# A two-layer hybrid decoder trunk on one core: gate and branch products token-major, weight prefetch raised in steps, a planner that orders by data dependencies, and the two parts of x side by side

## The chip, the core and the metric

The kernel runs on one core of one Trainium2 chip. The metric is the time of one execution on the device in microseconds (us). A core has a matrix engine (TensorE, "PE" in the profile, with its weight loads as "PEld"), a vector engine (VectorE, "DVE"), an activation engine (ScalarE, "ACT"), GpSimd ("POOL") and SyncE ("SP"), whose queue here issues nearly all DMAs. Each engine works through its own instructions in order; engines wait for one another through semaphores.

## The reference

Two layers, each a token mixer and a SwiGLU feed-forward part, on 256 tokens of 1024 channels, all in float32. What the change touches is the mixer's input projection (its merge gates), the three branch products and the output product:

```python
proj = jnp.einsum("bsd,de->bse", x, w_in)
...
gates = jax.nn.sigmoid(p_merge + gate_b).reshape(Bsz, S, N_BRANCH, D)
merged = sum(gates[:, :, gi] * jnp.einsum("bsc,cd->bsd", y, w_branch[gi])
             for gi, y in enumerate((ya, yb, yc)))
return jnp.einsum("bsd,de->bse", merged, w_out).astype(x.dtype)
...
x = _layer_norm(alpha * x + mix, ln1_g[l], ln1_b[l])
h = jax.nn.silu(jnp.einsum("bsd,df->bsf", x, w1)) * jnp.einsum("bsd,df->bsf", x, w3)
```

The branches are a gated linear recurrence (A), a chunked gated delta rule with a triangular solve (B) and chunked gated linear attention (C). `p_merge` has 3 x 1024 columns, each branch product is 512 by 1024.

## The kernel before

**Precision and weights.** A float32 product is made of three matmuls on values split in a high and a low part: high x high, high x low, low x high. Weights come in units of 128 x 1024 values (512 KB); `load_w` fetches a unit into one of 4 `raw` tiles over SP's queue, `split_w` makes the parts (`hi` by ACT, `lo` by DVE), and `unit` hands them to the matmuls. `fill` keeps `ahead[0]` units split ahead of use: 6, and 14 (`FAR`) from the first product of branch B on. All larger tiles share 37 slots of 128 x 1024 values (`slot`); PSUM is 8 banks of 128 x 512 values (`bank`).

**Two shapes of product.** Feature-major (`fm_acc`, output tile `fm` or `br`): the weights are stationary, the 256 tokens move, one matmul writes 128 features by 256 tokens. Token-major (`tm_acc`, output `tm`, `wo`, `w`): 128 tokens are stationary and 512 columns of weights move. Both do the same arithmetic per unit: 24 matmuls of 256 columns or 12 of 512. In the feed-forward part `fm_acc2` (output `f13`, named `f` in the trace) takes the high weights once for both parts of x, as 512 moving columns in two runs of 256 that lie 512 values apart (`xtile`, order q, k, c), and then the low weights with 256 columns.

**The mixer's order** stands in `MIX`. The units before the gates make the inputs of the branches. Each gate unit pair (`gA0` and so on, 4 for each branch, `fm_pair` with `g_chain`) ends in two sigmoids on ACT that read PSUM and add the bias as a per-partition operand. Each branch unit (`bA0`, with `m_chain`) ends in a product with its gate and a sum into `macc` on DVE; the last branch splits `macc` straight into `mh`, which the output product `wo` then uses as stationary operand, since it is feature-major already. Between these units stand the short steps of the chains (`b_inv`, `a_chain`, `c_chain`): a few small matmuls (`px`, `pp`, `pt`, `pw`, ...), then a copy or a product on ACT or DVE, and so on.

**What sets the order.** `Order` keeps a clock for each engine with a cost for each operation, and `drive` takes the next step of a chain as soon as its inputs are ready by these clocks, or else the next unit of the main stream. Within one step an operation is taken to wait for all that the other engines did in this step. ACT's functions that need a table (`TABLES`) are held in this order; a change of table costs an `ACT_TABLE_LOAD`.

Of the kernel before, what the change touches and what calls it, by code (L numbers as in the profile page):

```python
# [33 lines left out]
V_AW, V_AB, V_BR, V_BI, V_LAM, V_BW, V_BN, V_CG, V_CN, V_GB, V_AL, V_SM = (  # L34
    0, 16, 20, 24, 28, 32, 80, 81, 83, 84, 108, 112)
NV = 113
# [5 lines left out]
MIX = ("c0 c1 ax0 k0 k1 q0 z0 q1 ax1 v0 v1 ag0 ag1 gA0 gA1 gA2 gA3 bA0 bA1 bA2 bA3 "  # L42
       "gC0 bC0 gC1 bC1 gC2 bC2 gC3 bC3 gB0 gB1 bB0 bB1 gB2 bB2 gB3 bB3").split()
# [4 lines left out]
def stream_order():  # L48
# [5 lines left out]
    for u in MIX:  # L54
        nm, i = u[:-1], int(u[-1])
        if nm == "z":
            o += tm(C_Z)
        elif nm in base:
            o += fm(base[nm], i)
        else:  # L60
            b = "ABC".index(nm[1])
            o += fm(C_MG + 1024 * b, i) if nm[0] == "g" else [("br", b, i)]
    o += [("wo", n, q) for n in range(2) for q in range(4)]
# [11 lines left out]
def pack(inp):  # L75
# [3 lines left out]
    for l in range(L):  # L79
        w_in = a["w_in"][l]  # L80
        for i, u in enumerate(ORDER):
# [5 lines left out]
            elif u[0] == "br":  # L87
                src, sh = a["w_branch"][l, u[1]][:, 256 * q:256 * q + 256], (4, P, 256)
# [21 lines left out]
    for l in range(L):  # L110
# [11 lines left out]
        v[:, V_GB:V_GB + 24] = fm(a["gate_b"][l])  # L122
# [9 lines left out]
    for n, s in enumerate((8, 16)):  # L132
# [13 lines left out]
        "wg2": np.ascontiguousarray(a["c_w_g2"]),  # L146
        "lnv": np.ascontiguousarray(np.stack(
# [9 lines left out]
class Order:  # L157

    def __init__(self):
        self.clk = {e: 0.0 for e in ("pe", "act", "dve", "pool", "dma")}
        self.tok = {}
        self.chains = []
        self.table = "?"
        self.begin(0.0)

    def begin(self, ready):
        self.ready = ready
        self.fin = {}  # L170

    def op(self, eng, cost, ready=0.0):
        t = max([self.clk[eng], self.ready, ready] +
                [f for e, f in self.fin.items() if e != eng])
        t += cost
        self.clk[eng] = t
        self.fin[eng] = t
        return t

    def end(self):  # L180
        return max(list(self.fin.values()) + [self.ready])
# [67 lines left out]
def _build(ctx, nc, tc, ins, out):  # L249
# [33 lines left out]
    def act_fn(o, i, f, **k):  # L283
# [10 lines left out]
        O.op("act", 0.12 + 0.09 * aps + 0.000833 * n_of(o))  # L294
# [4 lines left out]
    def dve(o, x=0.0):  # L299
        O.op("dve", 0.13 + x + 0.00104 * n_of(o))  # L300

    def tt(o, a, b, op):
        V.tensor_tensor(out=o, in0=a, in1=b, op=op)  # L303
        dve(o)

    def ts(o, a, s1, op0, s2=None, op1=None):
# [4 lines left out]
        dve(o)  # L311

    def stt(o, a, s, b, op0, op1):
        V.scalar_tensor_tensor(out=o, in0=a, scalar=s, in1=b, op0=op0, op1=op1)
        dve(o, 0.06)

    def vcopy(o, i):
        V.tensor_copy(o, i)
        dve(o)

    def cpred(o, m, d):
        V.copy_predicated(o, m, d)
        dve(o)

    def rowsum(o, i):
        V.tensor_reduce(o, i, axis=AX.X, op=ADD)
        dve(i)

    def scan(o, a, b):
        V.tensor_tensor_scan(o, a, b, 0.0, MULT, ADD)  # L330
        dve(o, 0.00104 * n_of(o))

    def recip(o, i):
        V.reciprocal(o, i)
        dve(o, 0.0075 * n_of(o))

    def rsqrt(o, i, e):
        G.tensor_tensor(out=o, in0=i, in1=e, op=ALU.pow)
        O.op("pool", 0.3 + 0.17 * n_of(o))
# [5 lines left out]
    def mm(o, w, x, start=True, stop=True):  # L345
        T.matmul(o, w, x, start=start, stop=stop)  # L346
        n, m = n_of(x), n_of(w)
        if w.dtype == F32R:
            O.op("pe", max(n, m, 128) / 2400.0)
        else:  # L350
            O.op("pe", max(n, m, 32) / 600.0)

    def tp(o, i, idn):
        T.transpose(o, i, idn)  # L354
        O.op("pe", 0.107)
# [46 lines left out]
    def load_w(between=None):  # L402
# [5 lines left out]
        for c in halves(i):  # L408
            nc.sync.dma_start(out=t[:, c], in_=ins["w"][l, j][:, c])
            if i == 0 and c.start == 0:  # L410
                between()
        O.clk["dma"] = max(O.clk["dma"], O.clk["pe"] - 4.0) + 1.5
        raws.append((t, O.clk["dma"] + 2.0))

    def split_w(between=None):
        if not raws:
            return
        t, at = raws.pop(0)
        i = pos[1]
        pos[1] += 1  # L420
        keep = O.ready, O.fin
        O.begin(at)
# [8 lines left out]
        ready.append((hi, lo, O.end()))  # L431
        O.ready, O.fin = keep
        load_w()
# [7 lines left out]
    def unit(nk, hold=0):  # L441
# [4 lines left out]
        hi, lo, at = ready.pop(0)  # L446
        O.ready = max(O.ready, at)
# [5 lines left out]
    def fm_acc(o, w, x, c=slice(None)):  # L453

        nk = w[0].shape[1]
        for k in range(nk):
# [22 lines left out]
    def xtile(name):  # L479
        v = [slot(name, F32R).rearrange("p (q k c) -> p k q c", q=2, k=2) for _ in range(4)]  # L480
# [14 lines left out]
    def layer(l, xs, xtok):  # L495
# [507 lines left out]
        def g_chain(ps, b, j):  # L1003
            ps = p2(ps)
            if j % 2 == 0:
                B["gt", b, 0], B["gt", b, 1] = pair2("gt")
            gt = B["gt", b, j % 2]
            for t in range(2):
                act_fn(gt[:, t], ps[:, t], AF.Sigmoid, bias=vc(V_GB + 8 * b + 2 * j + t))
            B["gg", b, j] = gt  # L1010
            done(f"gt{b}{j}")
            return
            yield

        def m_chain(ps, n, b, j, mh, ml):
            yield k_(f"gt{b}{j}")
            ps = p2(ps)
            gt = B["gg", b, j]
            if n == 0:
                if j % 2 == 0:  # L1020
                    B["macc", j], B["macc", j + 1] = pair2("macc")
                tt(B["macc", j], ps, gt, MULT)
            else:
                tt(gt, ps, gt, MULT)
                tt(B["macc", j], B["macc", j], gt, ADD)
            if n == 2:
                split(mh[j], ml[j], B["macc", j])
                done(f"mrg{j}")

        def ln_chain(tk, halves, lv, xs_out, is_out, name):  # L1030
# [5 lines left out]
            for n, ps in enumerate(halves):  # L1036
# [5 lines left out]
                for c0 in range(sl.start, sl.stop, c):  # L1042
                    V.bn_stats(st[:, c0 // c], s[:, c0:c0 + c])
                    O.op("dve", 0.1 + 0.001 * c)
                c0 = sl.stop
            mv, rs = sm("mv", [P, 2]), sm("rs", [P, 1])
            V.bn_aggr(mv, st[:, 0:D // c].rearrange("p a b -> p (a b)"))
# [101 lines left out]
        def tm_group(x, chains, second):  # L1149


            if second is None:
                for chain in chains:
                    ps = [bank("tm") for _ in range(2)]
                    for q in range(4):
# [3 lines left out]
                        if q == 3:  # L1159
                            for tk in range(2):  # L1160
                                O.spawn(chain(ps[tk], tk), 1)
                        yield
                return
            u = []
            for tk in range(2):
                if tk:
                    yield second
                for n, chain in enumerate(chains):
                    ps = bank("tm")
                    for q in range(4):  # L1170
# [9 lines left out]
                        if q % 2:  # L1180
                            yield

        def fm_pair(chain, prio):
            ps = bank("fm")
            for t in range(2):
                fm_acc(p2(ps)[:, t], unit(8), xs)
                if t:
                    O.spawn(chain(ps), prio)
                yield

        def main():
# [17 lines left out]
            for u in MIX:  # L1209
# [11 lines left out]
                elif nm[0] == "g":  # L1221
                    b = "ABC".index(nm[1])
                    yield from fm_pair(lambda ps: g_chain(ps, b, i), 1)
                else:
                    n, b = BRANCHES.index(nm[1]), "ABC".index(nm[1])
                    if n == 2:
                        ahead[0] = FAR
# [3 lines left out]
                    w = unit(4)  # L1231
                    ps = bank("br")
                    for t in range(2):
                        fm_acc(p2(ps)[:, t], w, y, slice(P * t, P * t + P))
                    O.spawn(m_chain(ps, n, b, i, mh, ml), 1)
                    yield
# [18 lines left out]
            seq = [(n, q) for n in range(2) for q in range(4)]  # L1255
# [8 lines left out]
            for i in range(8 - tail):  # L1264
                yield k_(f"mrg{i}")
                w = unit(2)
                for tk in range(2):
                    wo(i, w, tk)
            u = []
            for tk in range(2):  # L1270
                for i in range(8 - tail, 8):
                    if tk == 0:
                        if i < 4:
                            yield k_(f"mrg{i}")
# [37 lines left out]
            for j in range(NF - tail):  # L1312
# [7 lines left out]
                yield  # L1320
# [25 lines left out]
    with tc.manual_schedule(engines={mybir.EngineType.SP}):  # L1346
# [9 lines left out]
        for q in range(4):  # L1356
            if q % 2 == 0:
# [3 lines left out]
            ld = [lambda c=c: nc.sync.dma_start(out=t[:, c:c + 3 - n],  # L1361
                                                in_=ins["xfm"][:, 2 * q + c:2 * q + c + 3 - n])
# [4 lines left out]
        nc.sync.dma_start(out=kc, in_=ins["kc"])  # L1367
        for l in range(L):
            nc.sync.dma_start(out=vecs[:, l], in_=ins["vec"][l])
# [4 lines left out]
        for l in range(L):  # L1374
            nc.sync.dma_start(out=wr[l], in_=ins["wsm"][l])
# [46 lines left out]
        def prep_aw(l):  # L1422
# [3 lines left out]
            for q in range(2):  # L1426
                ar = ars[q]
                G.memset(ar, 0.0)
                O.op("pool", 0.6)
                src = ins["aw"][l, q].rearrange("(c w) i j -> w i c j", w=2)  # L1430
                for w in range(2):
                    nc.sync.dma_start(out=h4(ar)[64 * w:64 * w + 64, :, 64 * w:64 * w + 64],
                                      in_=src[w])
            O.op("dma", 6.0)
# [5 lines left out]

        O.tok["xin"] = 0.0
# [18 lines left out]
```

## Time and profile before

| | us |
|---|---|
| median of 3 runs (lowest to highest) | 939.6 (938.99 to 940.14) |
| the profiled execution | 940.46 |
| its span, first to last instruction | 938.7 |
| PE busy in it | 924.4 |
| DVE busy | 642.0 |
| ACT busy | 527.6 |

The profile is of one execution. Busy times of PE are modelled and its matmuls overlap: the mean duration of a matmul is longer than the distance between two of them. The chain of waits gives a stretch of matmuls with its length and its count, and from that the distance. 1.8 us of the execution lie around the span.

### The profile page before, as it was taken

How to read it: one execution, taken by the hardware profiler on the slowest of the kernel's cores; microseconds unless marked ns; L12 is line 12 of the kernel's file. 1: busy time of each engine (PE TensorE's matmuls, PEld its weight loads, DVE VectorE, ACT ScalarE, POOL GpSimd, SP SyncE). 2: the span in 40 equal slices, each digit the busy share in tenths (PEclk: the TensorE clock that was granted, in tenths of full speed). 3: DMA queues.
4: the chain of work that ended last, by engine and by line, in shares of the span. 5: the costliest groups of instructions: out<-in, count | busy, mean ns of one | idle time of the engine just before them, and what ended most of it. 6: DMA issues, size and time to landing. Idle time of an engine off the chain costs nothing.

```text
span 938.7 us, 15760 instructions
## 1 busy us (share of the span) xinstructions
PE 924.4 (98%) x6306; PEld 840.3 (90%) x6306; DVE 642.0 (68%) x1017; ACT 527.6 (56%) x827; POOL 29.0 (3%) x29
## 2 busy tenths in 40 slices
PE   8999999999999999999999999999999999999996
PEld 5999999999988888888889999989999888888885
DVE  6778976675865776675557879574768658666715
ACT  5867679535724755565045864973457147555600
POOL 1000100000000000000000020000100000000001
PEclk9999999999999999999999999989999999999999
DMA  8855243545851865578144444234468248555801
GB/s 284 257 183 154 78 149 94 186 166 193 297 222 67 281 213 186 193 244 264 54 156 140 144 146 131 95 122 149 158 240 285 105 138 280 187 179 180 291 1 45
DMA packets 47993, 162.84 MB, mean 173 GB/s; under 512 B 7536, under 2 KB 8496, under 8 KB 47792
## 3 DMA queue, kind: packets, MB, share of 16 engines
q1 hardware_dynamic: 47776, 161.71, 51.5%
q8 instruction: 49, 0.80, 0.3%
q14 instruction: 24, 0.20, 0.1%
q10 hardware_dynamic: 144, 0.13, 0.0%
HBM read 160.77 MB, written 1.05 MB: 172 GB/s over the span
## 4 chain that ended last, share of the span: by engine, by line
PE 91%; ACT 4%; DVE 2%; DMA 1%; issue 1%; POOL 0%; SPq 0%; POOLq 0%; DVEq 0%; ACTq 0%
PE fm L346 25%; PE f L346 22%; PE w L346 13%; PE tm L346 11%; PE br L346 7%; PE wo L346 5%; DMA raw<-in_w_dram 1%; ACT L291 1%; PE pt L346 1%; PE pp L346 1%; DVE lo L303 1%; PE pln L354 1%; PE co L346 1%; ACT hi L291 1%; PE ptm L354 0%
## 5 line engine op out<-in xcount | busy, mean ns | idle before, releaser
L303 DVE TENSOR_TENSOR lo<-raw,hi 128x1024 fp32r<-128x1024 f32 (+1 forms) x293 | 350.8, 1217 | 94.4 <-ACT hi L291 88.1
L291 ACT ACTIVATE hi<-raw 128x1024 fp32r<-128x1024 f32 (+1 forms) x293 | 300.6, 1053 | 79.5 <-DMA raw<-in_w_dram 64.6
L346 PE MATMUL fm<-x,hi 128*128 128x256 f32 x1536 | 282.9, 286 | 0.0
L346 PEld LDWEIGHTS fm<-x,hi 128*128 128x128 f32 x1536 | 240.1, 192 | 2.3 <-issue 1.6
L346 PE MATMUL fm<-x,lo 128*128 128x256 f32 x768 | 217.6, 283 | 0.0
L346 PE MATMUL f<-x,hi 128*128 128x512 f32 x576 | 203.8, 399 | 0.0
L346 PE MATMUL f<-x,lo 128*128 128x256 f32 x576 | 161.8, 281 | 0.0
L346 PEld LDWEIGHTS fm<-x,lo 128*128 128x128 f32 x768 | 147.7, 192 | 0.0
L346 PEld LDWEIGHTS f<-x,hi 128*128 128x128 f32 x576 | 108.2, 188 | 26.9
L346 PE MATMUL w<-hi,hh 128*128 128x512 f32 (+1 forms) x396 | 111.1, 367 | 0.0
L346 PEld LDWEIGHTS f<-x,lo 128*128 128x128 f32 x576 | 108.8, 189 | 0.1
L346 PE MATMUL tm<-hi,x 128*128 128x512 f32 x320 | 100.7, 398 | 2.1 <-ACT hi L291 2.1
L346 PEld LDWEIGHTS w<-hi,hh 128*128 128x128 f32 x396 | 71.4, 189 | 12.3
L346 PEld LDWEIGHTS tm<-hi,x 128*128 128x128 f32 x320 | 59.3, 190 | 15.3 <-ACT hi L291 3.8
L346 PE MATMUL w<-lo,hh 128*128 128x512 f32 (+1 forms) x198 | 72.4, 366 | 0.0
L346 PE MATMUL tm<-lo,x 128*128 128x512 f32 x160 | 62.2, 392 | 0.1
L291 ACT ACTIVATE gt<-fm,vecs 128x256 f32<-128x256 f32 x48 | 20.5, 470 | 48.0 <-PE fm L346 48.0
L346 PEld LDWEIGHTS w<-lo,hh 128*128 128x128 f32 x198 | 37.3, 188 | 6.2
L291 ACT ACTIVATE x<-pln 128x256 fp32r<-128x256 f32 x24 | 7.9, 383 | 61.7 <-PE pln L354 61.7
L346 PE MATMUL wo<-hi,mh 128*128 128x512 f32 x128 | 39.8, 392 | 0.0
L303 DVE TENSOR_TENSOR hv<-f,hv 128x256 f32<-128x256 f32 x36 | 15.2, 422 | 31.4 <-ACT hv L291 31.4
L346 PEld LDWEIGHTS tm<-lo,x 128*128 128x128 f32 x160 | 30.2, 189 | 7.1 <-DVE lo L303 0.7
(276 smaller groups left out, 1081.8 us busy)
## 6 DMA issues: line engine op xcount, KB each, us to landing
raw<-in_w_dram SPq DMA_DIRECT2D x291, 512.0 KB, 4.4
lnv<-in_lnv_dram SPq DMA_DIRECT2D x8, 512.0 KB, 8.0
xr<-in_xtm_dram SPq DMA_DIRECT2D x1, 1024.0 KB, 7.4
xin<-in_xfm_dram SPq DMA_DIRECT2D x3, 256.0 KB, 7.0
raw<-in_w_dram SPq DMA_DIRECT2D x2, 256.0 KB, 3.4
ar<-in_aw_dram SPq DMA_DIRECT2D x8, 64.0 KB, 3.9
out_dram<-xr SPq DMA_DIRECT2D x2, 256.0 KB, 2.1
kc<-in_kc_dram SPq DMA_DIRECT2D x1, 476.0 KB, 8.9
```

What stands on the lines that cost most here:

```text
L291: ins_ = A.activation(o, i, f, **k)
L303: V.tensor_tensor(out=o, in0=a, in1=b, op=op)
L346: T.matmul(o, w, x, start=start, stop=stop)
L354: T.transpose(o, i, idn)
```

## The change

Gates and branch products become token-major: `gA0` is now 512 columns of gates for both halves of the tokens (4 units, 48 matmuls of 512 columns), `bA0` 512 columns of the product (2 units). `MIX` has two of each per branch in place of four. The gate's bias differs from column to column there, so that it is fetched as a tile of 128 equal rows (`gbias`, 512 KB, one for each branch and layer, on SP's queue) and added by DVE from PSUM; ACT then takes the sigmoid. The last branch's sum is token-major, and `m_tm` turns it by four matrix transposes for each half of the columns and of the tokens (`pmt`) before the split into `mh`. `wo` walks its units in the order of the columns of `mh`.

`ahead[0]` goes up by 1 at each unit of branch C and by 2 at each of branch B, and to 14 only at `wo`. `Order` now notes which part of which tile each operation reads and writes, so that an operation waits for its own inputs alone; its costs are new, an engine's occupation and the delay until a result can be read are kept apart, and DMA is counted by bytes. `fm_pair`, `tm_group` and the branch units yield after half a unit, so that chain steps can go between. `xtile` lays the parts of one block side by side (order k, q, c): `fm_acc2`'s 512 columns are now one run.

```diff
+MIX = ("c0 c1 ax0 k0 k1 q0 z0 q1 ax1 v0 v1 ag0 ag1 gA0 gA1 bA0 bA1 gC0 bC0 gC1 bC1 "
+       "gB0 gB1 bB0 bB1").split()
...
+            o += tm(C_MG + 1024 * b + 512 * i) if nm[0] == "g" else [
+                ("br", b, i, q) for q in range(2)]
+    o += [("wo", n, q) for q in range(4) for n in range(2)]
...
+    def op(self, eng, occ, tail=0.0, out=None, ins=(), ready=0.0):
+
+        t = max(self.clk[eng], self.ready, ready)
+        for a in ins:
+            t = max(t, self.after(eng, a, False))
+        if out is not None:
+            t = max(t, self.after(eng, out, True))
+        self.clk[eng] = t + occ
+        f = t + occ + tail
...
     def xtile(name):
-        v = [slot(name, F32R).rearrange("p (q k c) -> p k q c", q=2, k=2) for _ in range(4)]
+        v = [slot(name, F32R).rearrange("p (k q c) -> p k q c", q=2, k=2) for _ in range(4)]
...
+        def g_tm(ps, b, j, tk, bias):
+            if tk == 0:
+                B["gt", b, j] = pair("gt")
+            gt = B["gt", b, j][tk]
+            tt(gt, ps, bias[:, 512 * j:512 * j + 512], ADD)
+            yield
+            act_fn(gt, gt, AF.Sigmoid)
+            done(f"gt{b}{j}{tk}")
...
+            tt(gt, ps, gt, MULT)
+            acc = B["macc", tk][j]
+            tt(acc, acc, gt, ADD)
+            if n == 1:
+                return
+            yield
+            pt = h4(bank("pmt"))
+            for q in range(4):
+                tp(pt[:, q], acc[:, q * P:(q + 1) * P], ident)
+            for q in range(2):
+                split(*(x[2 * j + q][:, :, tk * P:(tk + 1) * P] for x in (mh, ml)),
+                      pt[:, 2 * q:2 * q + 2])
+            done(f"mrg{j}{tk}")
...
-                    yield from fm_pair(lambda ps: g_chain(ps, b, i), 1)
+                    if i == 0:
+                        bias = slot("gbias")
+                        nc.sync.dma_start(out=bias, in_=ins["gb"][
+                            l:l + 1, 1024 * b:1024 * b + 1024].to_broadcast([P, 1024]))
+                    yield from tm_group(xs, [
+                        lambda ps, tk: g_tm(ps, b, i, tk, bias)], None)
...
+                    if n == 1:
+                        ahead[0] = min(ahead[0] + 1, FAR)
                     if n == 2:
-                        ahead[0] = FAR
+                        ahead[0] = min(ahead[0] + 2, FAR)
```

How the instructions stand on three engines, before and after. First PE at the end of the mixer of layer 0 (`br`: last branch product, `ybh`: branch B's output, `wo`: the output product's four banks, `mh`: the merged sum). Before the change:

```order
L346 MATMUL br_3121<-ybh_2483,hi_2851 128x256 x2
L346 MATMUL br_3121<-ybh_2483,lo_2852 128x256
L346 MATMUL wo_3161<-hi_2857,mh_375 128x512 x2
L346 MATMUL wo_3161<-lo_2858,mh_375 128x512
L346 MATMUL wo_3161<-hi_2857,mh_375 128x512 x2
```

After it, at the same place:

```order
L389 MATMUL br_2651<-hi_2518,ybh_2233 128x512 x2
L389 MATMUL br_2651<-lo_2519,ybh_2233 128x512
L398 MATMUL pmt_2721<-kc_73,macc_2096 128x128 x4
L398 MATMUL pmt_2730<-kc_73,macc_2130 128x128 x4
L398 MATMUL pmt_2741<-kc_73,macc_2096 128x128 x4
L389 MATMUL wo_2713<-hi_2541,mh_377 128x512
L389 MATMUL wo_2715<-hi_2541,mh_377 128x512
L389 MATMUL wo_2714<-hi_2559,mh_377 128x512
L389 MATMUL wo_2713<-hi_2541,mh_377 128x512
L389 MATMUL wo_2713<-lo_2542,mh_377 128x512
```

The transposes of the last sums now stand between the last branch product and `wo`; the first matmuls of `wo` take three banks in turn. Then ACT in layer 1, where the recurrence of branch A (`th`, `a`, `r`, `v` and `gl` are its and branch B's inputs) meets the steps of the solve (`pb` and `X` are copies out of PSUM that the next small matmuls `pt` and `pp` wait for; `hi` is a weight split). Before:

```order
L291 ACTIVATE r_6441<-a_6443 128x512 x2
L291 ACTIVATE hi<-raw 128x1024
L291 ACTIVATE pb<-pp 128x512
L291 ACT_TABLE_LOAD
L291 ACTIVATE gt<-fm,vecs 128x256 x2
L291 ACTIVATE pb<-pp 128x512
L291 ACTIVATE hi<-raw 128x1024
L291 ACTIVATE gt<-fm,vecs 128x256 x2
L291 ACT_TABLE_LOAD
L291 ACTIVATE th<-th 128x512 x2
L291 ACTIVATE hi<-raw 128x1024
L291 ACTIVATE X<-px 128x512 x2
```

After it, at the same step of the solve:

```order
L331 ACTIVATE v<-fm,vecs 128x256 x2
L331 ACTIVATE hi<-raw 128x1024
L331 ACTIVATE pb<-pp 128x512 x2
L331 ACTIVATE th<-r_5845,nc_81 128x256 x4
L330 ACT_TABLE_LOAD
L331 ACTIVATE a_5847<-r_5845,nc_81 128x256 x4
L331 ACTIVATE r_5845<-a_5847 128x512 x2
L331 ACT_TABLE_LOAD
L331 ACTIVATE v<-v 128x512
L331 ACTIVATE hi<-raw 128x1024
L331 ACTIVATE X<-px 128x512 x2
L331 ACTIVATE hi<-raw 128x1024
```

Both copies of `pb` now stand together ahead of the loads of tables, and no gate's sigmoid (`gt`) stands in this stretch. Last SP's queue in layer 0 (`raw`: weight units, `ar`: small weights of the next layer). Before:

```order
L409 DMA raw<-in_w_dram 128x1024 x14
L1432 DMA ar<-in_aw_dram 64x4x64 x4
L409 DMA raw<-in_w_dram 128x1024 x35
L1432 DMA ar<-in_aw_dram 64x4x64 x4
L409 DMA raw<-in_w_dram 128x1024 x36
L1249 DMA xr<-in_xtm_dram 128x2048
```

After it, up to the fetch of `xr` again:

```order
L447 DMA raw<-in_w_dram 128x1024 x13
L447 DMA ar<-in_aw_dram 64x4x64 x4
L447 DMA raw<-in_w_dram 128x1024 x28
L1284 DMA gbias<-in_gb_dram 128x1024
L447 DMA raw<-in_w_dram 128x1024 x8
L447 DMA ar<-in_aw_dram 64x4x64 x4
L447 DMA raw<-in_w_dram 128x1024 x4
L1284 DMA gbias<-in_gb_dram 128x1024
L447 DMA raw<-in_w_dram 128x1024 x14
L1284 DMA gbias<-in_gb_dram 128x1024
L447 DMA raw<-in_w_dram 128x1024 x16
L1317 DMA xr<-in_xtm_dram 128x2048
```

Three fetches of `gbias` now stand between the weight units, each as the first gate of its branch begins.

## Rows read from the trace of the kernel before

**Rows 1.** The page: busy time per engine; shares of the chain by engine.

```profile
PE 924.4 (98%) x6306; PEld 840.3 (90%) x6306; DVE 642.0 (68%) x1017; ACT 527.6 (56%) x827; POOL 29.0 (3%) x29
...
PE 91%; ACT 4%; DVE 2%; DMA 1%; issue 1%; POOL 0%; SPq 0%; POOLq 0%; DVEq 0%; ACTq 0%
```

**Rows 2.** The chain, in order of time: start us, us, engine, output, count of matmuls.

```profile
32.48 2.88 PE fm L346 x24
...
113.47 0.87 PE px L354 x8
...
178.93 8.63 PE br L346 x72
...
222.98 11.52 PE fm L346 x96
...
257.54 19.97 PE wo L346 x88
...
309.72 96.10 PE f L346 x544
...
478.60 10.91 PE tm L346 x48
...
491.37 2.86 PE fm L346 x24
...
615.36 3.95 PE fm L346 x24
...
721.16 8.21 PE wo L346 x36
...
869.70 61.09 PE w L346 x330
```

**Rows 3.** Busy time by stretch: stretch, length, PE, PEld, DVE, ACT, POOL, PEclk, DMA.

```profile
92.70:120.00 27.30, 27.30 (x228) 26.82 (x227) 26.75 (x64) 17.76 (x33) 4.65 (x2) 1.00 0.31 110
120.00:150.00 30.00, 29.57 (x315) 28.92 (x315) 18.40 (x30) 25.92 (x45) 0.00 (x0) 1.00 0.33 98
150.00:257.50 107.50, 107.50 (x913) 107.10 (x913) 77.21 (x100) 63.62 (x86) 2.63 (x3) 1.00 0.60 201
580.00:616.00 36.00, 33.47 (x269) 32.98 (x268) 22.65 (x30) 32.41 (x50) 0.00 (x0) 0.93 0.37 122
616.00:656.00 40.00, 39.94 (x407) 39.16 (x406) 24.73 (x38) 20.34 (x34) 0.00 (x0) 0.98 0.45 145
```

**Rows 4.** Timeline of PE, 610 to 616 us: two waits for ACT.

```profile
610.64 1.90 PE L346 MATMUL pt<-pb,X 128*128 128x128 f32 x8 [1.79 <-ACT pb L291]
613.28 2.08 PE L346 MATMUL pt<-pb,X 128*128 128x128 f32 x8 [0.74 <-ACT pb L291]
```

**Rows 5.** Timeline of ACT, 605 to 613.5 us: what its copies of pb queue behind.

```profile
605.12 1.28 ACT L290 ACT_TABLE_LOAD   x1
606.41 1.71 ACT L291 ACTIVATE a<-r,nc 128x256 f32<-128x256 f32 x4
...
610.02 0.57 ACT L291 ACTIVATE pb<-pp 128x512 f32<-128x512 f32 x1
610.61 1.28 ACT L291 ACT_TABLE_LOAD   x1
611.90 0.84 ACT L291 ACTIVATE gt<-fm,vecs 128x256 f32<-128x256 f32 x2
612.63 0.60 ACT L291 ACTIVATE pb<-pp 128x512 f32<-128x512 f32 x1
```

**Rows 6.** Groups of instructions by form: count, busy us, mean ns, idle before.

```profile
L303 DVE TENSOR_TENSOR gt<-br,gt 128x512 f32<-128x512 f32 x16 | 11.0, 685 | 3.9 <-PE br L346 3.9
...
L303 DVE TENSOR_TENSOR x<-pln,x 128x256 fp32r<-128x256 f32 x24 | 9.0, 416 | 11.7 <-ACT x L291 11.7
...
L303 DVE TENSOR_TENSOR mh<-macc,mh 128x512 fp32r<-128x512 f32 x8 | 5.5, 685 | 0.0
```

**Rows 7.** The page, DMA issues: count, KB each, median us to landing.

```profile
lnv<-in_lnv_dram SPq DMA_DIRECT2D x8, 512.0 KB, 8.0
```

More of the change, by code (lines that the diff above doesn't have):

```diff
@@ L163, in __init__ @@
         self.tok = {}
+        self.mem = {}
         self.chains = []
@@ L400, in halves, with dma, load_w @@
         return [slice(c, c + n) for c in range(0, 1024, n)]
-    def load_w(between=None):
+    def dma(o, i, free=0.0):
+        nc.sync.dma_start(out=o, in_=i)
+        O.clk["dma"] = max(O.clk["dma"], free + 1.5)
+        keep, O.ready, last = O.ready, 0.0, O.last
+        f = O.op("dma", o.shape[0] * n_of(o) * 4 / 285e3, 0.5, o)
+        O.ready, O.last = keep, last
+        return f
+    def load_w(between=None, free=0.0):
         i = len(raws) + pos[1]
@@ L417, in split_w @@
             return
-        t, at = raws.pop(0)
+        t = raws.pop(0)
         i = pos[1]
         pos[1] += 1
-        keep = O.ready, O.fin
-        O.begin(at)
+        keep = O.ready, O.last
+        O.begin(0.0)
         hi, lo = slot("hi", F32R), slot("lo", F32R)
@@ L430, in split_w @@
         tt(lo_, t_, hi_.bitcast(F32), SUB)
-        ready.append((hi, lo, O.end()))
-        O.ready, O.fin = keep
-        load_w()
+        ready.append((hi, lo))
+        at = O.end()
+        O.ready, O.last = keep
+        load_w(free=at)
     held, ahead = [0], [AHEAD]
@@ L451, in xk, with fm_acc @@
         return x[k // 2][:, k % 2]
-    def fm_acc(o, w, x, c=slice(None)):
+    def fm_acc(o, w, x, k0, k1, c=slice(None)):
         nk = w[0].shape[1]
-        for k in range(nk):
+        for k in range(k0, k1):
             mm(o, w[0][:, k, c], xk(x[0], k), k == 0, False)
@@ L1185, in fm_pair @@
             for t in range(2):
[L1186 to L1189, printed above, removed]
+                w = unit(8)
+                for k in range(0, 8, 4):
+                    fm_acc(p2(ps)[:, t], w, xs, k, k + 4)
+                    if t and k:
+                        O.spawn(chain(ps), prio)
+                    yield
         def main():
@@ L1230, in main @@
                     y = B[y]
[L1231 to L1236, printed above, removed]
+                    ps = [bank("br") for _ in range(2)]
+                    for q in range(2):
+                        w = unit(2)
+                        for tk in range(2):
+                            tm_acc(ps[tk], y, tk, w, 2 * q, q == 0, q == 1)
+                            if q:
+                                O.spawn(m_tm(ps[tk], n, b, i, tk, mh, ml), 1)
+                            yield
                 seen.append(u)
@@ L1254, in main @@
                 O.spawn(ln_chain(tk, pw[tk], lv, x1, False, "x1"), 0)
-            seq = [(n, q) for n in range(2) for q in range(4)]
+            ahead[0] = FAR
+            seq = [(n, q) for q in range(4) for n in range(2)]
             def wo(i, w, tk):
```

168 lines of the change are left out of this document (87 added, 81 removed).

## The prediction

> **What bounds the kernel now.** I read the page first: PE is busy for 98% of the span and holds 91% of the chain that ended last, while DVE and ACT have 68% and 56% [rows 1]. So the kernel's time is the number of matmuls times their distance, plus what PE waits. Distances come from the chain of waits, where a stretch of matmuls stands with length and count [rows 2]. Gates: 11.52 us for 96 matmuls of 256 columns, 120.0 ns each. Branch products: 8.63 for 72, 119.9 ns. Token-major: 10.91 for 48 matmuls of 512 columns, 227.3 ns. Twice 120.0 is 240.0, so 512 columns are 12.7 ns cheaper in one matmul than in two. In the feed-forward part 544 matmuls of `f` take 96.10 us, 353.3 ns for each pair of one matmul of 512 columns and one of 256.
>
> Then I looked for what PE waits. The two layers do the same mixer work, from the first `fm` to the first `wo`: 257.54 - 32.48 = 225.06 us in layer 0 and 721.16 - 491.37 = 229.79 in layer 1 [rows 2]. Layer 1 loses 4.7 us more. The table by stretch says where: between 580 and 616 us PE is busy for 33.47 of 36 us and the granted clock falls to 0.93, with ACT busy for 32.41; everywhere else in the mixers at most 0.43 us of PE is idle, in 120 to 150 [rows 3]. The timeline shows two steps `pt` of the solve waiting 1.79 and 0.74 us for `pb` on ACT [rows 4], and ACT's own shows why: the copies of `pb`, 0.6 us each, stand behind table loads of 1.28 us, `a` and the gates' sigmoids `gt` [rows 5]. After these waits the clock is at the lower of its two levels (1.2 against 2.4 GHz) for a moment: 24 matmuls `fm` take 3.95 us where 2.88 is usual [rows 2].
>
> **Token-major gates and branch products.** A gate group is now 4 units of 12 matmuls, a branch group 2 of 12. Before there were 2 layers x 24 units x 24 = 1152 matmuls for gates and 2 x 12 x 24 = 576 for branches, 1728 of 256 columns; now there are 864 of 512. 1728 x 120.0 ns = 207.4 us against 864 x 227.3 ns = 196.4: **11.0 us less** on PE, all on the path [rows 2]. The new products have the form of `tm`, whose row is the price, so the bound from both sides is narrow: with `wo` as the row (19.97 for 88, 226.9 ns) it is 11.3, and one wait of 0.1 us at each of 24 groups would leave 8.6.
>
> The Trainium skill (TensorE: Matmul & The Clock Gate, Back-to-back issue gap) gives N/2.4 + 2.5 ns as the distance of a matmul alone. By it two of 256 columns would cost 218.4 and one of 512 215.8, so the gain would be an estimated 2.2 us. The rows above differ: each matmul here carries 13 to 14 ns beyond its columns, and the measurement decides.
>
> **Transposes of the merged sum.** 2 layers x 4 groups x 4 = 32 transposes are new on PE. Eight transposes `px` take 0.87 us [rows 2], 0.11 each: **3.5 us more**. At the entry of `wo` they stand ahead of all of its matmuls, as the listing in the change shows. DVE has four products of 0.685 us for the last group [rows 6], of which the first can start with the end of the first bank, 6 matmuls or 1.36 us before PE is through with the second. They end 4 x 0.685 - 1.36 = 1.4 us after the last branch matmul, a split of 0.42 behind them [rows 6] makes 1.8; PE has 12 transposes (1.3) and three `wo` on high parts (0.7) meanwhile, 2.0. So I put 0.1 us per layer there, with 0 and 1.4 (the cover of the transposes gone) as ends.
>
> **x parts side by side.** The pair of `f` reads its 512 columns in two runs. In the last layer's `w`, 198 matmuls of 512 columns in one run are mixed with 132 of 256: 198 x 227.3 + 132 x 120.0 = 60.8 us against the row's 61.09 [rows 2], so that next to each other they keep their distances. A pair should then take 347.3 instead of 353.3 ns; 576 pairs give **3.5 us less**. The ends: nothing, if the two runs aren't what costs 6 ns, and 5.2, if the whole 9 ns in `f`'s longer matmul go.
>
> **The new order in layer 1.** With the order of the listing both `pb` come ahead of the tables, and the gates' sigmoids come later. What is late next is the copy of X and the `v` that branch B transposes. From the second `pb` on ACT does `th` (1.7, as `a`), a table (1.28), `a` (1.71), squares (1.1), a table (1.28) and a silu (0.6): 7.7 us. PE has meanwhile `pt` (16 small matmuls, 1.8), a unit of `fm` (2.88), `px` (0.87) and half a unit (1.44): 7.0 [rows 2, 5]. So about 0.8 us of wait remain of the 4.7, at worst all 4.7 (another step takes their place); 0 is the other end. **3.9 us less.** The 0.43 us of layer 0 I leave.
>
> **Work beside the path.** DVE gains 24 bias additions from PSUM, bounded by the products from PSUM at 0.685 us, and 16 splits of 0.42 for 8 of 0.685: 16.4 + 1.2 = 17.6 us [rows 6]. Half falls to each layer, in a stretch where DVE is busy for 77.21 of 107.50 us [rows 3]; 86 of 102 is cover enough. ACT's sigmoids do not become more. If that cover goes, each group of gates or branches waits for its two products, 1.4 us (first rival). `gbias` is a fetch of 512 KB like `lnv`, 8.0 us from issue to landing [rows 7]. It is read after a group's first half, at the earliest 9.5 us (42 matmuls) after the group begins, and the `raw` fetches queued behind it on SP have 6 split units, 6 x 2.73 = 16.4 us of matmuls, before PE needs them. I take nothing; uncovered, each of the 6 would cost up to its 8.0 us. Raising the prefetch in steps moves splits, it adds none: nothing, with the small matmuls' copies on ACT as those who would wait.
>
> **The sum.** 11.0 - 3.5 + 3.5 + 3.9 - 0.2 = 14.7 us. The profiled execution took 940.46 us, 1.8 of it around the span and 0.9 above the median; against the span that is 924.0, against the median **939.6 - 14.7 = 924.9 us**. Its own range is 921.5 to 928.
>
> **Rivals.**
> - *DVE holds the banks (slower).* A gate group ends in two additions on DVE, a branch group in two to four products, each behind weight splits in an engine that works in order; PSUM has 8 banks and every group takes two. In 92.7 to 120 us DVE is busy for 26.75 of 27.30 [rows 3]. If each of the 24 groups makes PE wait for two such products, 1.37 us, that is 32.9 us: 939.6 - 14.7 + 32.9 = 957.8. It decides from 0.61 us a group on. Against it: the full stretch lies ahead of the gates, and between a group's end and the next use of its banks lie two more groups, over 10 us.
> - *The waits only move.* The order gives back 4.7 us at one place and takes the same at others, since ACT keeps its table loads and the chains still run through it: 939.6 - 11.0 + 0.2 = 928.8. For it: it is an order computed from clocks, as the one before was.
> - *The two runs don't cost.* The change then leaves `f` at 353.3 and doesn't do what it says there: 928.4.
> - *More goes than I count.* 9 ns in place of 6 at `f` (1.7 us), no wait left in either layer (1.4): 924.9 - 3.1 = 921.8.
> - *A distance by columns alone.* If a matmul of 256 columns took half of 227.3 ns in these places, the gain of 11.0 us would be nothing: 939.6 - 3.7 = 935.9. The 120 ns of `fm`, of `br` and of the last layer's `w` speak against it [rows 2]. By the rule of the Trainium skill above (the same page and section) it would come near this, at an estimated 933.7.
>
> **How the numbers follow.** Forecast 0.52, waits that only move 0.18, more than I count 0.11, two runs 0.08, distance by columns 0.02, DVE 0.09. In DVE's case I give 0.04 to a time that ends within 0.2% of 939.6 and 0.05 to a slower one; 0.2% is about what a measurement of this kernel can tell from no change. All others are faster by more: 0.91. The range goes from 920.5 (more than I count, with some slack) to 931 (waits that move, with 2 us for a cost unseen); outside are DVE's case, the distance by columns and tails of the others, 0.2.
>
> **What would show it.** Right: 864 matmuls `tm` and `br` at 227 ns, pairs of `f` at 347, `pmt` at 0.11 us each, a granted clock of 1.00 in layer 1's mixer, the mixers of both layers equally long within 1 us. Wrong: PE waiting for DVE at `tm` or `br`, ACT waiting for DVE at the sigmoids with small matmuls queued behind, `lo` waiting for `gbias`, or pairs of `f` still at 353.

## The result, and the profile after

The changed kernel takes 925.25 us in the median (four runs, 924.97 to 926.49); the kernel before, measured beside it on the same chip, takes 939.87. The ratio is 0.9834, with a 95% interval of 0.9817 to 0.9852. The forecast was 924.9.

The page of the profiled execution (925.02 us, span 923.3), answering to [rows 1] and [rows 7]: busy time with counts, the chain by engine, the new fetch of `gbias` (count, KB, us to landing).

```profile
PE 911.3 (99%) x5474; PEld 794.7 (86%) x5474; DVE 657.7 (71%) x1049; ACT 517.4 (56%) x806; POOL 27.2 (3%) x29
...
PE 98%; DMA 1%; DVE 0%; issue 0%; SPq 0%; ACT 0%; POOL 0%; POOLq 0%
...
gbias<-in_gb_dram SPq DMA_DIRECT2D x6, 512.0 KB, 4.8
```

PE's share of the chain goes from 91% to 98%: the pieces that led through ACT and DVE are gone. The chain, answering to [rows 2] (start us, us, what, count of matmuls):

```profile
204.24 10.88 PE tm L389 x48
...
242.32 10.88 PE br L389 x48
253.21 1.31 PE pmt L398 x12
254.52 4.22 PE wo L389 x18
258.74 0.44 PE pmt L398 x4
...
301.18 5.65 PE f L389 x32
306.83 0.44 PE pht L398 x4
307.27 94.30 PE f L389 x544
```

Gates (`tm`) and branch products (`br`) go at 226.7 ns, 16 transposes take 1.75 us a layer, and the 544 `f` take 94.30 us for 96.10, 346.7 ns a pair. The table by stretch, answering to [rows 3] (the second row lies over the solve of layer 1; both engine columns and PEclk as there):

```profile
150.00:257.00 107.00, 107.00 (x532) 89.36 (x532) 86.79 (x118) 58.45 (x74) 2.62 (x3) 1.00 0.68 231
570.00:606.00 36.00, 36.00 (x348) 33.79 (x346) 26.15 (x45) 30.74 (x51) 1.64 (x1) 1.00 0.29 102
```

PE is busy for all of both stretches, the clock stays at 1.00 in layer 1's solve, and DVE is busy for 86.79 of 107 us beside the gates. Of the waits of [rows 4] none is left. What PE waits for in the whole execution (us in total, times, longest) are two rows, both of the start (`warm`: warm-up matmuls; `tm`: the first weight units):

```profile
PE tm L389 <- ACT hi L331: 2.6, 2, 2.0
PE warm L1423 <- DVE warm L1420: 1.2, 1, 1.2
```

To see where time went, I cut each profiled execution at the first matmul of every stage. Each entry is the distance between two such matmuls in us (start: up to the first `fm`; mixer: from there to the first `wo`; `wo`: to the first `f`; `f`: to the first `w`):

| kernel | start | mixer 0 | wo 0 | f 0 | mixer 1 | wo 1 | f 1 |
|---|---|---|---|---|---|---|---|
| before | 32.31 | 225.07 | 46.09 | 102.18 | 229.79 | 46.35 | 102.18 |
| after | 34.21 | 220.06 | 46.75 | 100.38 | 219.82 | 46.78 | 100.38 |
| x_adjacent_alone | 35.72 | 225.07 | 46.10 | 102.18 | 230.30 | 46.03 | 102.18 |
| x_apart | 33.42 | 220.04 | 46.73 | 100.38 | 219.82 | 46.76 | 100.38 |
| odd_columns | 34.23 | 225.07 | 46.09 | 101.43 | 230.16 | 47.17 | 101.75 |
| planner_alone | 34.11 | 224.30 | 46.07 | 100.37 | 224.06 | 46.33 | 100.38 |
| token_major_alone | 33.42 | 220.43 | 46.64 | 100.38 | 226.42 | 47.23 | 102.18 |
| whole_turns | 33.87 | 220.74 | 46.69 | 100.38 | 220.54 | 46.71 | 100.38 |
| prefetch_jump | 32.89 | 227.16 | 47.76 | 100.38 | 226.30 | 48.18 | 102.18 |
| prefetch_late | 34.05 | 221.36 | 54.71 | 102.18 | 221.09 | 52.76 | 100.38 |
| no_turn | 34.93 | 218.85 | 47.91 | 100.38 | 218.57 | 47.91 | 100.38 |
| bias_add_2x | 32.76 | 220.09 | 47.53 | 100.38 | 220.06 | 47.30 | 100.38 |
| bias_add_4x | 33.32 | 228.78 | 46.75 | 100.38 | 228.51 | 48.19 | 100.38 |
| filled_start | 33.43 | 220.06 | 46.81 | 100.38 | 219.80 | 46.79 | 100.38 |

From before to after: mixers -5.01 and -9.97, `wo` +0.66 and +0.43, `f` -1.80 twice, start +1.90; the stages left out differ by 0.2. That is the 15.4 us between the two spans. Each row is one execution; the start differs between executions of the same order of work too (before 32.31, x_adjacent_alone 35.72), so its +1.90 can't be put down to the change.

### The profile page after: what moved, and what is told of

It is laid out like the page before. It is cut to its first block, busy times and chain, and to the rows that moved or that the text cites. A ratio compares the mean times of both kernels' runs of the same rounds, so it can differ in the third digit from the quotient of the medians.

```text
span 923.3 us, 14086 instructions
## 1 busy us (share of the span) xinstructions
PE 911.3 (99%) x5474; PEld 794.7 (86%) x5474; DVE 657.7 (71%) x1049; ACT 517.4 (56%) x806; POOL 27.2 (3%) x29
## 4 chain that ended last, share of the span: by engine, by line
PE 98%; DMA 1%; DVE 0%; issue 0%; SPq 0%; ACT 0%; POOL 0%; POOLq 0%
PE tm L389 26%; PE f L389 22%; PE fm L389 15%; PE w L389 13%; PE br L389 7%; PE wo L389 5%; PE pt L389 1%; PE pp L389 1%; DMA raw<-in_w_dram 1%; PE pln L398 1%; PE pr L389 1%; PE ptm L398 1%; PE px L398 1%; PE co L389 1%; PE pss L389 0%; PE pat L389 0%
## 5 line engine op out<-in xcount | busy, mean ns | idle before, releaser
L389 PE MATMUL tm<-hi,x 128*128 128x512 f32 x704 | 221.8, 397 | 2.6 <-ACT hi L331 2.6
L389 PE MATMUL f<-x,hi 128*128 128x512 f32 x576 | 200.2, 392 | 0.0
L389 PEld LDWEIGHTS tm<-hi,x 128*128 128x128 f32 x704 | 130.7, 190 | 30.4 <-ACT hi L331 4.3
L389 PE MATMUL fm<-x,hi 128*128 128x256 f32 x768 | 142.0, 286 | 0.0
L389 PE MATMUL tm<-lo,x 128*128 128x512 f32 x352 | 137.6, 392 | 0.1
L389 PEld LDWEIGHTS fm<-x,hi 128*128 128x128 f32 x768 | 119.6, 191 | 1.8 <-issue 1.6
L389 PE MATMUL fm<-x,lo 128*128 128x256 f32 x384 | 108.6, 283 | 0.0
L389 PEld LDWEIGHTS tm<-lo,x 128*128 128x128 f32 x352 | 66.5, 189 | 15.0 <-DVE lo L346 0.7
L389 PEld LDWEIGHTS fm<-x,lo 128*128 128x128 f32 x384 | 73.5, 191 | 0.0
L357 DVE SCALAR_TENSOR_TENSOR xr<-xr,w 128x512 f32<-128x512 f32 (+1 forms) x9 | 5.6, 627 | 38.7 <-PE w L389 38.7
```

## Experiments

All are timed beside the kernel before. The theory on record is the prediction's sum. Its weak points were the reason for `f`'s gain, the cover on DVE, the layer-1 wait, and the prefetch costed at nothing.

### Where x's parts lie

x_adjacent_alone is the kernel before with only this edit; x_apart is the kernel after with only this edit undone:

```
-        v = [slot(...).rearrange("p (q k c) -> p k q c", q=2, k=2) for _ in range(4)]
+        v = [slot(...).rearrange("p (k q c) -> p k q c", q=2, k=2) for _ in range(4)]
```

> The kernel before with one edit: the two parts of x side by side. The order of PE's instructions is that of before. Theory (the two runs cost the 6 ns): pairs of f at 347 ns instead of 353, 576 of them, 3.5 us less, about 936.2. Rival (the runs don't cost): pairs stay at 353 and the time at 939.7. Second rival: the whole 9 ns of f's longer matmul go, 344 a pair and 5.2 us less, 934.5.

> The kernel after, with the parts of x apart again (q ahead of k in a slot), so that the 512 moving columns of f are two runs of 256. Side by side earns it: the 576 pairs go back from 346.7 to 353.3 ns, f takes 102.18 us a layer for 100.38, 925.25 + 3.6 = 928.9 us. The spacing has nothing to do with where the parts lie (as it stayed at 353.3 ns when they were laid side by side in the kernel before): 925.3 us, within 0.7, with f at 100.38 us in both layers.

Measured: x_adjacent_alone 942.05 us against 941.65, ratio 1.0001 (0.9987 to 1.0014); x_apart 924.77, ratio 0.9828 (0.9814 to 0.9841). The edit does nothing either way. The chain of x_adjacent_alone keeps 96.10 us for 544 `f`, with all 512 columns in one run:

```profile
313.13 96.10 PE f L346 x544
...
777.24 96.10 PE f L346 x544
```

So the rival "the two runs don't cost" was right that they don't, and yet `f` did get faster. The column `f` of the table shows how: in planner_alone, with x apart, both layers have 100.38; in token_major_alone and prefetch_jump layer 0 has 100.38 and layer 1 102.18; in prefetch_late it is the other way round. The same code of `f` takes either of two times. Which of them goes with the program and not with the layout: x_adjacent_alone repeats before's 102.18 in both layers and x_apart after's 100.38. In every trace that I read there, the first 32 `f` of a layer take 5.64 or 5.65 us (353 ns a pair), as in the chain of after above; four transposes `pht` then interrupt the stream, and behind them it goes on at one of two distances. That suggested a rhythm into which a stream of matmuls falls.

odd_columns puts ten extra matmuls into the kernel before:

```
+ODD = ({6: 272, 9: 264, 12: 264, 15: 260, 18: 268},
+       {6: 264, 9: 272, 12: 260, 15: 260, 18: 260})
...
-                    fm_acc2(ps, unit(8), x1)
+                    w = unit(8)
+                    if chain is f_gate and f in ODD[l]:
+                        n = ODD[l][f] // 2
+                        T.matmul(ps[:, :, 0:n], w[0][:, 0], x1[2][0][:, 0][:, :, 0:n],
+                                 start=True, stop=True)
+                    fm_acc2(ps, w, x1)
```

> The kernel before with 10 more matmuls in f, five in a layer, each ahead of a group of f, six groups apart, of 272, 264, 264, 260 and 268 columns in layer 0 and 264, 272, 260, 260 and 260 in layer 1 (their result is overwritten). 10 x 0.12 = 1.2 us more. The 353.3 ns of a pair is a rhythm into which the stream of matmuls has fallen when it starts, and which a matmul of odd length can shift: behind at least one of the ten the pairs go on at another distance, 346.7 ns (832 for 848 cycles of 2.4 GHz), and behind 272 columns, a multiple of 16, nothing changes. It is the place of x's parts, the slots or the banks: 353.3 ns all through, 939.9 + 1.2 = 941.1 us. If all pairs behind the first odd one went over, f would be 100.7 to 101.3 us a layer and the total 938 to 939.5.

Measured: 940.62 us, ratio 0.9997 (0.9986 to 1.0008). The chain, layer 0 and then layer 1; the extra matmuls stand between the rows:

```profile
305.55 5.65 PE f L347 x32
311.63 5.65 PE f L347 x32
317.41 16.65 PE f L347 x96
334.18 16.64 PE f L347 x96
350.94 16.96 PE f L347 x96
368.02 16.65 PE f L347 x96
384.79 22.19 PE f L347 x128
769.81 5.65 PE f L347 x32
775.89 5.65 PE f L347 x32
781.67 16.66 PE f L347 x96
798.45 16.96 PE f L347 x96
815.52 16.65 PE f L347 x96
832.29 16.96 PE f L347 x96
849.37 22.19 PE f L347 x128
```

96 `f` are 48 pairs: 16.96 us is 353.3 ns a pair, 16.65 is 346.9, and 22.19 for 64 pairs is 346.7. Eight of the ten extra matmuls switch the distance, in both directions; the second (264 columns) and the last (268) of layer 0 do not. x's slots and layout are the same all along a layer, and banks and weight slots rotate as they did before the edit, so these don't set it. Shown is that the stream has two distances and that one extra matmul can switch between them; "rhythm" is my name for it, and which length switches it isn't understood. Nor is it known what in the new program made the stream take the faster one behind `pht`. I had expected 272 columns to change nothing, and both matmuls of 272 switched it. What in the chip keeps the rhythm stays open. The Trainium skill (TensorE: Matmul & The Clock Gate, Back-to-back issue gap) gives N/2.4 + 2.5 ns as the distance of a matmul alone; by it a pair would take an estimated 325 ns. The trace disagrees: both its values, 346.7 and 353.3, lie above that.

### The planner and the token-major work, each alone

planner_alone is the kernel after with before's gates, branches, unit list, jump of the prefetch and x layout. token_major_alone is the kernel before with after's gates, branches, merge, unit list and steps of the prefetch, under before's planner. In short, seen from after and from before:

```
planner_alone
-                    yield from tm_group(xs, [lambda ps, tk: g_tm(ps, b, i, tk, bias)], None)
+                    yield from fm_pair(lambda ps: g_chain(ps, b, i), 1)
token_major_alone
-                    yield from fm_pair(lambda ps: g_chain(ps, b, i), 1)
+                    yield from tm_group(xs, [lambda ps, tk: g_tm(ps, b, i, tk, bias)], None)
```

> The kernel before with the planner of the change alone: dependencies by tile, its costs, and turns of half a unit; gates and branches feature-major, prefetch and x as before. Theory (the order took the waits of layer 1 away): layer 1's mixer as long as layer 0's to within 1 us, granted clock 1.00 there, 4.7 us less, about 935.0. Rival (waits only move): mixers of 225 and 230 us or the same sum with the wait elsewhere, 939.7. Third reading: part of the gain needs the sigmoids gone from that stretch, then 1 to 3 us less.

> The kernel before with token-major gates and branches, gbias, the transposes and the stepped prefetch, but the planner before and x as before. Theory (the terms add): 11.0 less from 864 matmuls at 227 ns for 1728 at 120, 3.5 more from transposes, layer 1's wait of 4.7 stays or moves: about 932.4. Rival (the new work needs the new order): waits at gates, branches or the entry of wo of 5 us and more, 937 or over. Second rival (the old order happens to lose its wait with the moved sigmoids): 928.

Measured: planner_alone 932.04 us against 941.65, ratio 0.9896 (0.9883 to 0.9908); token_major_alone 932.41, ratio 0.9903 (0.9887 to 0.9920). The planner alone takes 0.8 us from layer 0's mixer and 5.7 from layer 1's, more than the 4.7 by which layer 1 had been longer; layer 1's mixer is now as long as layer 0's to 0.24 us, as the theory said. In all it lost 9.6 us where the theory has 4.7; 3.6 of them are `f`, which the theory didn't count. From planner_alone to after both mixers lose 4.24 us: token-major work, 1.31 us of transposes among it. token_major_alone lost 9.2 us against before's 941.65 beside it, where its theory has 7.5; 1.8 of them are `f` in layer 0, and the rest is what the theory says. Without the new planner the old wait is back; PE's timeline of token_major_alone:

```profile
606.45 2.49 PE L348 MATMUL pt<-pb,X 128*128 128x128 f32 x16 [2.85 <-ACT pb L293]
```

whole_turns asks what in the planner does it. It keeps the order from data dependencies and undoes the half-unit turns:

```
-                            yield
+                        yield
```

(so in the token-major groups and in `br`, and in the same way for the k halves in `fm_pair`; a group with a second part yields every second unit)

> The kernel after with turns as long as before's: the planner is asked after every whole unit (24 matmuls of fm, 12 of tm and br), and in the groups with a second part after every second unit; its order still comes from the data that operations touch. The dependencies alone took layer 1's wait and the rest of the 5.7 us away: 925.3 us, within 0.7, mixers of 219.8 to 220.5 us. The half turns did it: the small solve's steps stand up to 2.9 us late again, PE waits for DVE in layer 1, 928 to 931 us.

Measured: 925.95 us, ratio 0.9840 (0.9824 to 0.9856). Its mixers are 0.7 us longer each, 220.74 and 220.54. Half turns are worth that. The rest of the 6.5 us then belongs to what is left of the new planner, the order from data dependencies and the new costs; neither was undone by itself, so which of the two gives it is not shown.

### The prefetch

Before raised the prefetch from 6 to 14 units ahead at its first product B. after goes up by one and by two units at its branches and to 14 at `wo`. prefetch_late raises only at `wo`:

```
                     n, b = BRANCHES.index(nm[1]), "ABC".index(nm[1])
-                    if n == 1:
-                        ahead[0] = min(ahead[0] + 1, FAR)
-                    if n == 2:
-                        ahead[0] = min(ahead[0] + 2, FAR)
```

prefetch_jump has these lines in their place, and so raises at once at the same product as before:

```
+                    if n == 2:
+                        ahead[0] = FAR
```

> The changed kernel with the prefetch of before: 6 units ahead until the first product of branch B, then 14 at once. Theory (the steps move splits and add none; PE has 6 units in hand): within 1 us of the changed kernel, 925.3. Rival (the jump floods ACT, DVE and the slots): waits of PE in the stretch of branch B, 2 us or more longer, 927.5 and over.

> The kernel after without the two steps: 6 units ahead up to wo, 14 from there. Raised at once at the first product B, the prefetch had cost 16 us. If that came only from the splits that stood ahead of the last sums on DVE, not raising it costs nothing in the mixers (219.8 to 220.1 us); 925.3 us, within 0.7. If the steps are needed, wo and f begin with too few units ready: PE waits for hi or lo in wo or in the first groups of f, 1 to 6 us, 926.5 to 931 us, and less than the jump's.

Measured: prefetch_jump 941.37 us, ratio 0.9996 (0.9985 to 1.0007); prefetch_late 941.71, ratio 1.0006 (0.9994 to 1.0018). Either way the whole gain is gone: by the table mixers and `wo` together are 16.0 and 16.5 us longer than in after, and one layer's `f` another 1.8. The jump went the way of its rival, with many times the 2 us named there; the late raise lies outside both readings, and PE waits at another place than the second one said. In prefetch_jump PE waits for the last sums; PE's timeline, then DVE's:

```profile
251.75 0.60 PE L398 MATMUL pmt<-kc,macc 128*128 128x128 f32 x4
256.63 1.12 PE L398 MATMUL pmt<-kc,macc 128*128 128x128 f32 x4 [4.28 <-DVE macc L346]
```

```profile
250.70 1.22 DVE L346 TENSOR_TENSOR lo<-raw,hi 128x1024 fp32r<-128x1024 f32 x1
251.83 1.28 DVE L346 TENSOR_TENSOR gt<-tm,gbias 128x512 f32<-128x512 f32 x2
253.03 1.21 DVE L346 TENSOR_TENSOR lo<-raw,hi 128x1024 fp32r<-128x1024 f32 x1
254.16 0.68 DVE L346 TENSOR_TENSOR gt<-br,gt 128x512 f32<-128x512 f32 x1
254.76 1.21 DVE L346 TENSOR_TENSOR lo<-raw,hi 128x1024 fp32r<-128x1024 f32 x1
255.90 0.68 DVE L346 TENSOR_TENSOR macc<-macc,gt 128x512 f32<-128x512 f32 x1
```

Weight splits of 1.2 us stand before the bias additions, products and sums on DVE, so the last `macc` end 4 us late. In prefetch_late the splits come one stage on, in the layer norm behind `wo`. Its PE timeline, then its DVE's:

```profile
282.96 1.76 PE L398 MATMUL pln<-kc,xr 128*128 128x128 f32 x7 [5.02 <-DVE xr L357]
```

```profile
274.99 1.22 DVE L346 TENSOR_TENSOR lo<-raw,hi 128x1024 fp32r<-128x1024 f32 x1
276.12 0.69 DVE L1100 BATCH_NORM_STATS2 st<-xr 128x6 f32<-128x512 f32 x1
277.50 1.23 DVE L346 TENSOR_TENSOR lo<-raw,hi 128x1024 fp32r<-128x1024 f32 x1 [0.69 <-ACT hi L331]
278.64 0.20 DVE L1105 BATCH_NORM_AGGREGATE mv<-st 128x2 f32<-128x12 f32 x1
278.76 0.63 DVE L357 SCALAR_TENSOR_TENSOR xr<-xr,wo 128x512 f32<-128x512 f32 x1
279.64 1.23 DVE L346 TENSOR_TENSOR lo<-raw,hi 128x1024 fp32r<-128x1024 f32 x1 [0.24 <-ACT hi L331]
```

The waits cost clock as well. Behind the wait of prefetch_late (columns as in [rows 3]):

```profile
283.00:289.00 6.00, 6.00 (x18) 4.69 (x19) 5.86 (x13) 1.32 (x4) 0.99 (x1) 0.51 0.20 73
```

6 us at 0.51 do the work of 3.06, so that 5.02 us of wait cost an estimated 7.96, just what `wo` of layer 0 is longer (54.71 for 46.75). The steps put the splits in between, where the gates and the products of C and B run and DVE has room: in after it is busy for 30.3 of the 40 us from 200 to 240 and makes 20 splits there, against 18 in prefetch_jump and 16 in prefetch_late. The jump by itself does no harm: planner_alone keeps it, and PE waits for DVE nowhere in its mixers. It costs beside the work that token-major gates and sums put on DVE.

### Cover on DVE, and the transposes

bias_add_2x repeats the bias addition of each gate half-group once, bias_add_4x three times (`range(3)`); no_turn splits the merged sum as it stands:

```
bias_add_2x
             tt(gt, ps, bias[:, 512 * j:512 * j + 512], ADD)
+            for _ in range(1):
+                tt(gt, ps, bias[:, 512 * j:512 * j + 512], ADD)
no_turn
-            pt = h4(bank("pmt"))
-            for q in range(4):
-                tp(pt[:, q], acc[:, q * P:(q + 1) * P], ident)
+            pt = h4(acc)
```

> The kernel after with each bias addition of a gate group done twice: 24 x 0.69 = 16.5 us more on DVE, 8.2 us a layer. DVE's idle time covers them: 925.3 to 926.3 us. DVE holds the banks or the sums: up to 925.25 + 16.5 = 941.7 us, with PE's waits on tm or on macc; the clock halving after a wait as in the run with the prefetch raised at once would add some 2 us a layer.

> The kernel after with each bias addition done four times: 3 x 16.5 = 49.4 us more on DVE, 24.7 a layer, where twice had cost 1.1 us by its stretches. DVE idles some 20 us between the first gate and the end of the mixer in layer 0 (150 to 256 us), so 4 to 5 us a layer are uncovered, and the tail behind the last product grows by 3 x 0.69 for each addition there: 932 to 945 us, with PE's waits at pmt and wo, or at tm for banks. If the cover is wider than the stretch, because the splits move ahead: under 928 us. If banks are held, 24 groups x 2.06: up to 974 us.

> The kernel after without the transposes pmt: mh is split straight from the token-major sum, so what is computed isn't the reference's. As predicted for them, 32 x 0.11 us on the path: 925.25 - 3.5 = 921.7 us, the stretch from the last branch matmul to f shorter by 1.75 us a layer. They hide a wait for the last sum, which then shows in their place: 924 to 925.3 us, PE waiting for DVE ahead of wo. They cost more than their length (waits, banks): under 920.5 us.

Measured: bias_add_2x 926.57 us, ratio 0.9858 (0.9840 to 0.9877); bias_add_4x 944.51, ratio 1.0037 (1.0023 to 1.0051); no_turn 926.07, ratio 0.9850 (0.9830 to 0.9870). What PE waits for (us in total, times, longest), the rows of bias_add_2x, of bias_add_4x and of no_turn:

```profile
PE wo L389 <- DVE mh L346: 0.9, 2, 0.6
```

```profile
PE pmt L398 <- DVE macc L346: 10.9, 5, 4.0
```

```profile
PE wo L389 <- DVE mh L346: 3.2, 2, 1.6
```

16.5 us more on DVE cost 1.3 us in the median, where the intervals overlap, and 1.6 by the table, 1.3 of it in `wo`: DVE is busy for 11.9 of the 12 us from 240 to 252 (10.3 in after), so that the last sums and splits queue there. 49.4 us more cost 19: PE waits 10.9 us for the last sums, and the clock behind these waits is low (0.56 from 258 to 264 us); a wait for a bank at `tm` or `br` doesn't show. So the cover is wide in the middle and near nothing at the end. no_turn gives nothing back: the mixers and `wo` together take 266.76 and 266.48 us for 266.81 and 266.60. The 1.75 us of transposes a layer lie where PE would otherwise wait 1.6 us for the split of the last sum.

### The start

filled_start is the kernel after with warm-up matmuls in the wait for the second weight unit (the order of the matmul ahead of them and of the one behind is pinned):

```
                                 O.spawn(chain(ps[tk], tk), 1)
+                            if tk and pwarms:
+                                pwarm = pwarms.pop()
+                                for _ in range(8):
+                                    i = T.matmul(pwarm, warm[:, 0:P], warm, start=True, stop=True)
+                                    tc.stamp_issue_order_token(i.ins, "start")
```

> The kernel after with 8 more warm-up matmuls (bf16, 512 columns, 8 x 0.21 us) between the first unit's matmuls and the second's, where PE waits 2.0 to 3.3 us for the second weight unit. In 4 of 10 profiled executions the granted clock was 0.50 for some us behind that wait, and the start up to the first fm took 34.1 to 35.7 us, where it took 32.3 to 33.4 in those with the clock at 1.00. If the pause is what lets the clock fall: 1.00 behind it, a start of 32.3 to 33.4 us, and 924.3 us in the median, 0.9 below the kernel after. If the landing of the first transfers sets the start, the same 925.3 us; if the warm-ups stand in the way, 926.

Measured: 924.25 us (923.96 to 924.34), ratio 0.9821 (0.9805 to 0.9837). From 14 to 16 us, first after and then filled_start (columns as in [rows 3]):

```profile
14.00:16.00 2.00, 2.00 (x6) 1.52 (x6) 1.62 (x3) 1.06 (x1) 0.00 (x0) 0.50 0.71 207
```

```profile
14.00:16.00 2.00, 2.00 (x11) 1.62 (x10) 1.58 (x3) 1.06 (x1) 0.00 (x0) 1.00 0.65 160
```

In 7 of the 13 other profiled executions the clock falls behind that wait and the start takes 33.9 to 35.7 us; in the six others, with 1.00, it takes 32.3 to 33.4. The filled one kept the clock and started in 33.43, which one profile in six of thirteen would have done without it. More telling is the mean granted clock of each run: 0.997 or 0.998 in all four here, 0.995 or 0.996 in all four of after, and in x_apart 924.14 and 924.19 us at 0.998 but 925.36 and 925.88 at 0.995. The four filled runs lie 0.6 us or more below all four of after, but the two were not run side by side, and the intervals of the two ratios overlap: a version at least as good as after, whose 1.0 us isn't proved.

## Why the prediction was right, and where it was not

- **Token-major gates and branches, -11.0: right.** 864 matmuls at 226.7 ns are 195.9 us for 207.4; planner_alone against after gives 2 x (4.24 + 1.31) = 11.1 (the stepped prefetch differs between these two as well).
- **Transposes, +3.5, and the entry of `wo`, +0.2: right as time on PE.** They stand in the chain with 1.75 us a layer, and `wo` grew by 0.66 and 0.43, of which 0.44 each is the last four. The cover I named is real: without them PE waits 1.6 us, near the 1.4 given as the end of that term. But 3.5 us is no price that leaving them out would return.
- **x parts side by side, -3.5: the size came (-3.6), the reason was wrong.** The failed step is "a pair should then take 347.3 instead of 353.3 ns", read from `w`'s mix of lengths. The layout has no part in it; the new program fell into the faster rhythm in both layers. The low end, "nothing, if the two runs aren't what costs 6 ns", was the true price of the edit. The forecast for `f` hit for no reason that it gave: that is luck. Its other end, 5.2 us, took 9 ns off the longer matmul, where the rows leave 353.3 - 120.0 - 227.3 = 6.
- **The new order, -3.9: mechanism right, size too small.** It gave 6.5 us. The failed step is "What is late next": 7.7 us on ACT against 7.0 on PE should have left 0.8 of wait, and layer 1's solve shows none. The 0.43 us of layer 0 that I left aside gave 0.8, and layer 1 lost about as much again. This part of "more goes than I count" happened.
- **DVE's 17.6 us beside the path: right.** DVE's busy time grew by 15.7. Behind the warm-up PE waits for DVE nowhere in after. ACT idles 21.0 us for `gt` before its sigmoids, as feared, and no matmul waits for that. The rival named 0.61 us a group as its point; with 1.37 us more in each of the 12 gate groups (bias_add_2x), 16.5 in all, the loss is 1.3 to 1.6 us. The place that decides is the tail of the mixer, not the banks.
- **Prefetch in steps, "moves splits, adds none: nothing": the weakest line.** The sentence named ACT's copies as those who would wait and no price for a lost cover. Raised at once or late, the same splits cost 16 us. The edit keeps the other gains rather than adding one.
- **Not in the sum: the start**, +1.90 us in the profiled pair (the clock, above). Without it that pair lost 17.3 us where the sum has 14.7: the order was underrated by 2.6. So that the median came within 0.4 us of the forecast is in part luck: a miss in the order, and in after a start with a low clock that points the other way. How the starts of before went in the runs beside it isn't known.

## What to carry to other kernels

When an engine that works in order carries both bulk work (weight splits) and short steps on the path, a change in when the bulk is requested moves no work and still decides the result: price it by what stands behind the bulk at each place where it could land. A difference of a few per cent in the distance of the same matmuls isn't explained by the operand's layout until that layout alone has been changed; look first whether the same code shows both values in one trace. And work that stands in the chain isn't thereby worth its length: ask what PE would wait for if it were gone.

## What the runs showed of the hardware

- A steady stream of alternating fp32r matmuls of 512 and 256 columns runs at 346.7 or at 353.3 ns a pair, 1.9% apart. It keeps its distance for as long as nothing interrupts it (96.10 us in one piece), and a single extra matmul can switch it in either direction.
- An extra matmul of 272 columns, the one length that I had expected to change nothing, switched it both times; the four of 260 did so too, the one of 268 did not, and 264 did in two of three.
- In prefetch_late a wait of 5 us left the granted clock at 0.51 over the next 6 us, which adds an estimated 3 us to the wait's price (6 x 0.49); in the start, a wait of 2 to 3 us was followed by a lower clock in 7 of 13 executions.
